# Input-projection tiles and the LRU output projection trade places as filling of a chunked RWKV-7 recurrence

## The chip, the cores and the metric

One NeuronCore of one Trainium2 chip runs the whole layer as one program. The metric is the device time of one execution in microseconds. The kernel before took 3132.44 us (median of 3 runs, 3130.93 to 3138.77).

## What is computed

The reference is one layer of a diffusion backbone. A latent of 1024 tokens and a context prefix of 256 tokens, 1024 channels each, are normalised and projected by `w_in`. Two token mixers work on the result: an RG-LRU (convolution, gates, a scan over time, 1280 channels, both directions) and an RWKV-7 recurrence (16 heads of 64, both directions, whose state after the context seeds the latent's). Each has its output projection and a gate; their sum goes through `w_out`, and a SwiGLU follows. Cut to what matters here:

```python
def merge(lru, rwkv, g_lru, g_rwkv, p):
    m = jax.nn.sigmoid(g_lru) * (lru @ p['w_o_lru']) + jax.nn.sigmoid(g_rwkv) * (rwkv @ p['w_o_rwkv'])
    return m @ p['w_out']

def mixer(h_ctx, h_lat, p, rows, need_ctx_out):
    ux_c, uy_c, zr_c, gl_c, gr_c = jnp.split(h_ctx @ p['w_in'], pts, axis=-1)
    ux_l, uy_l, zr_l, gl_l, gr_l = jnp.split(h_lat @ p['w_in'], pts, axis=-1)
    ...
    lru_l = ((hf_l + hb_l) * jax.nn.gelu(uy_l)).astype(h_lat.dtype)
    rw_c, S_c = rwkv_branch(centred_shift(zr_c, p['rwkv_mu']), S_zero, p, need_ctx_out)
    rw_l, _ = rwkv_branch(centred_shift(to_colmajor(zr_l, rows), p['rwkv_mu']), S_c, p, True)
    out_l = merge(lru_l, rw_l, gl_l, gr_l, p)
```

The columns uy (LRU gelu branch), gl and gr (the two merge gates) of the projection are needed only by `lru_l` and `merge`.

## The kernel before

All products with float32 data are made of three matmuls of a split operand (hi*hi, hi*lo, lo*hi). Channels lie on the partitions, tokens on the free axis.

The first stage (`phase_ux`, line 243) projects the ten ux tiles, then V, and runs the LRU tile by tile beside that (`lru_tiles`, line 344, an interleaved generator). The second stage (`phase_a2`, line 808) makes the RWKV operands in ten units (two for the context, eight for the latent; four operand groups each, `wkv_operands`), and the 32x32 triangular inverses of each chunk on VectorE (`wkv_inverse`, line 702: 31 steps of two instructions, tiles `it` and `X`, then transposes into `xo` and stores into `x_d`, line 740). The last unit's inverse can start only when its operands are done.

The remaining 26 tiles of the projection (10 of uy, 8 of gl, 8 of gr) need nothing but `h`. `plain` (line 289) is a generator that does one such tile per call: `inproj` (line 218) loads two halves of the weight (256 KB each, `wraw`), splits them on VectorE (line 230) and GpSimd (line 231), makes 48 matmuls of 512 columns (two weight halves, two token halves, four blocks of channels, three products; tile `pin`), and ScalarE copies the two results into `ev` (line 296), which SyncE stores (line 297). `NFILL` = 15 of these tiles stand in the first stage, the last three (`NEND`) at its end; the other 11 are spread evenly over the second stage by a due rule (line 869), 11/38 of a tile per operand group.

The recurrence (`phase_b`, line 1118) has 40 steps of 32 tokens: 0 to 7 for the context, 8 to 39 for the latent. Two halves of the heads (`wkv_chain`, line 977) take turns: products `ru` of the chunk's keys with the state, a copy, a product with the chunk's inverse `xc`, copies, products `pn` for the next state, copies (line 985, or a VectorE multiply, line 1043, on odd steps), and for latent steps the outputs `py`, copied into `ys` and stored. Every step loads 1.5 MB (`skb`, `ska`) into rings of three steps (`wkv_load`, line 965). Step 8 is the first that needs the latent's inverses (`x_d`). Context steps have a high priority in the planner (`CTXP`, `CTXO`), which otherwise orders each engine's queue by its own time model and by the order in which the program was written.

Between the chain's pieces, twice a step (`FILLAT`), the LRU output projection is put in as filling (`lru_out`, line 1053): for each half of the tokens ten tiles are prepared (load `lh` and `lu`, gelu, product on GpSimd at line 1067, split at lines 68 and 69), then for eight output tiles 30 matmuls each (tile `pol`, line 1087), 480 in all. The pace counts context steps twice, and leaves `TAIL` = 45 for after the last step. From step 28 on the group norms of the recurrence's output (`norms`) join in.

Memory pools are stacked from two edges. `h`, the weight ring (`wpool`), `ev` (`evp`) and the projection's PSUM (`psin`) stay open until the end of the second stage; the recurrence's pool `bp` then takes their place. The inverse's pool `pinv` stands at the right edge from the second context unit on.

Of the kernel before, what the change touches and what calls it, by code (L numbers as in the profile page):

```python
# [8 lines left out]
F32 = mybir.dt.float32  # L9
# [7 lines left out]
P = 128  # L17
# [265 lines left out]
NFILL = 15  # L283
# [5 lines left out]
def plain(k, start=0):  # L289

    jobs = [(UY0 + i, k.uy_d, i) for i in range(10)]
    jobs += [(GL0 + i, k.gl_d, i) for i in range(8)] + [(GR0 + i, k.gr_d, i) for i in range(8)]
    for m, dst, i in jobs[start:]:
        for o, c, w in inproj(k, m, k.psin, LAT):
            u = k.evp.tile([P, 512], F32, name=f"ev{m}_{c}", tag="ev", bufs=EVB)
            k.nc.scalar.copy(u, o)
            k.nc.sync.dma_start(dst[i * P:(i + 1) * P, c:c + w], u)
        yield

# [508 lines left out]
def phase_a2(k, hc):  # L808
# [3 lines left out]
    with tc.tile_pool(name="pprep", bufs=1) as k.prep, tc.tile_pool(name="pzr", bufs=1) as k.zrp, tc.tile_pool(name="pa2c", bufs=1) as cp, \  # L812
# [106 lines left out]
EVB = 2  # L919
# [57 lines left out]
def wkv_chain(k, a):  # L977
# [13 lines left out]
    def outputs(s, tvu):  # L991
# [6 lines left out]
        ys = k.op.tile([P, 256], F32, name=f"ys{s}_{a}", tag="ys", bufs=4)  # L998
# [97 lines left out]
FILL0 = 0  # L1096
# [21 lines left out]
def phase_b(k):  # L1118
    tc = k.tc
    k.gnp = k.root.enter_context(tc.tile_pool(name="gnp", bufs=1, side="right"))  # L1120
    with tc.tile_pool(name="bp", bufs=1) as k.bp, tc.tile_pool(name="olp", bufs=1) as op, \
            tc.tile_pool(name="psc1", bufs=1, space=PSUM) as k.psb, tc.tile_pool(name="psc2", bufs=1, space=PSUM) as k.psb2, \
            tc.tile_pool(name="pso", bufs=1, space=PSUM) as pso:
        k.bpool = k.bp
        k.op = op
        fill = lru_out(k, op, pso)
        k.pe_after = None
        done = 0
        for _ in range(FILL0):
            next(fill)  # L1130
# [5 lines left out]
        halves = [wkv_chain(k, a) for a in range(2)]  # L1136
        for s in range(NSTEP + 1):
            for i, a in enumerate((0, 0, 1, 0, 1, 1, 0, 1)):
# [15 lines left out]
                if i in FILLAT:  # L1154
                    at = s + (FILLAT.index(i) + 1) / len(FILLAT)
                    while done < (480 - FILL0 - TAIL) * (at + CTXW * min(at, 8)) / (NFEND + 8 * CTXW):
                        next(fill, None)
                        done += 1
# [7 lines left out]
        k.pe_after = None  # L1166

# [513 lines left out]
```

## Time and profile before

| | |
|---|---|
| median of 3 runs | 3132.44 us |
| the profiled execution | 3125.42 us |
| its span | 3123.3 us |
| PE, VectorE, ScalarE, GpSimd busy | 87%, 61%, 47%, 32% |
| DMA, mean over the span | 137 GB/s |

The span is that of the hardware profile; the profiled execution's own time is 2.1 us more. Busy time of PE includes the drain of each matmul, so a busy PE is not a PE at its peak. "PEclk" is TensorE's granted clock as a share of full speed.

### The profile page before, as it was taken

The numbers are of one execution on the slowest core, as the hardware profiler recorded it, in microseconds if no ns is written. First come the engines' busy times: TensorE is split into PE (matmuls) and PEld (weight loads), VectorE is DVE, ScalarE is ACT, GpSimd is POOL, SyncE is SP. The second block draws the span as 40 slices with busy tenths as digits, with TensorE's granted clock in tenths as the row PEclk, the third lists the DMA queues.
The fourth block names the chain that finished last, engine by engine and source line by source line (L and its number), as shares of the span: only waits on it lengthen the run. The fifth ranks groups of instructions, "written<-read, shape, count | busy, mean of one in ns | idle before, by whom it ended". The sixth has DMA issues, their size and how long they took to land. (4 is left out here: it accounts for less than half of the span.)

```text
span 3123.3 us, 57216 instructions
## 1 busy us (share of the span) xinstructions
PE 2730.1 (87%) x22526; PEld 2168.8 (69%) x22526; DVE 1904.5 (61%) x2841; ACT 1454.4 (47%) x2645; POOL 1011.7 (32%) x896
## 2 busy tenths in 40 slices
PE   5988888889898878887898888677899999999998
PEld 4776666767776666765665666455678888888888
DVE  7688898985567887888755233455786323232234
ACT  3476777782467555767323343344434111111114
POOL 4344444452445545666315230335441000000000
PEclk9999999999999978987558998889999999999999
DMA  5333433422555455565858787888773211111112
GB/s 204 94 117 124 121 118 117 123 69 78 152 143 140 114 123 128 129 141 130 199 137 235 227 263 225 247 235 254 258 252 110 71 54 51 41 54 42 48 56 72
DMA packets 379603, 429.19 MB, mean 137 GB/s; under 512 B 134166, under 2 KB 286150, under 8 KB 371398
## 3 DMA queue, kind: packets, MB, share of 16 engines
q1 hardware_dynamic: 379334, 425.53, 47.3%
q8 instruction: 178, 2.92, 0.4%
q14 instruction: 91, 0.75, 0.1%
HBM read 286.87 MB, written 126.26 MB: 132 GB/s over the span
## 5 line engine op out<-in xcount | busy, mean ns | idle before, releaser
L88 PE MATMUL pin<-h1024hi,whi 128*128 128x512 f32 (+1 forms) x1024 | 431.2, 421 | 58.2 <-DVE whi L230 20.4
L90 PE MATMUL pin<-h1024hi,wlo 128*128 128x512 f32 (+1 forms) x1024 | 424.4, 418 | 11.8 <-POOL wlo L231 11.4
L89 PE MATMUL pin<-h1024lo,whi 128*128 128x512 f32 (+1 forms) x1024 | 426.1, 416 | 4.1 <-DVE h1024lo L120 4.1
L231 POOL TENSOR_TENSOR wlo<-wraw,whi 128x512 fp32r<-128x512 f32 (+1 forms) x144 | 212.8, 1478 | 309.9 <-DVE whi L230 153.7
L88 PEld LDWEIGHTS pin<-h1024hi,whi 128*128 128x128 f32 (+1 forms) x1024 | 204.0, 199 | 113.1 <-DVE whi L230 21.1
L90 PEld LDWEIGHTS pin<-h1024hi,wlo 128*128 128x128 f32 (+1 forms) x1024 | 203.3, 199 | 66.9 <-POOL wlo L231 19.1
L89 PEld LDWEIGHTS pin<-h1024lo,whi 128*128 128x128 f32 (+1 forms) x1024 | 203.6, 199 | 50.8 <-DVE h1024lo L120 6.6
L54 ACT ACT_TABLE_LOAD x164 | 210.4, 1283 | 28.7 <-DMA olg<-gl_d 12.1
L982 PE MATMUL pn<-tvu,ska 128*64 128x64 f32 (+1 forms) x2496 | 165.5, 253 | 36.7 <-ACT tvu L985 22.8
L1429 DVE TENSOR_TENSOR sil<-sil,pfu 128x512 f32<-128x512 f32 x44 | 30.3, 688 | 243.6 <-PE pfu L90 243.6
L982 PEld LDWEIGHTS pn<-tvu,ska 128*64 128x64 f32 (+1 forms) x2496 | 125.0, 158 | 75.0 <-ACT tvu L985 26.9
L388 DVE SCALAR_TENSOR_TENSOR lxc<-lup,c_lru_conv_w,lxc 120x512 f32<-120x512 f32 (+3 forms) x198 | 161.0, 837 | 16.8 <-ACT lxc L386 16.2
L1437 DVE SCALAR_TENSOR_TENSOR x<-pfo,modv,x 128x512 f32<-128x512 f32 (+1 forms) x112 | 74.2, 671 | 132.3 <-PE pfo L90 132.3
L985 ACT COPY tvu<-ru 32x256 f32<-32x256 f32 x193 | 69.9, 363 | 141.1 <-PE ru L982 72.8
L68 ACT CAST whi_fi<-wraw_fi 128x1024 fp32r<-128x1024 f32 x48 | 50.6, 1053 | 168.6 <-PE pfg L89 53.3
L720 DVE TENSOR_TENSOR it<-bp,X 128x62 f32<-128x62 f32 (+25 forms) x186 | 116.6, 627 | 4.1
L230 DVE CAST whi<-wraw 128x512 fp32r<-128x512 f32 (+1 forms) x144 | 77.5, 539 | 66.0 <-PE pin L89 27.7
L721 DVE TENSOR_TENSOR X<-X,it 128x62 f32<-128x62 f32 (+25 forms) x186 | 114.3, 614 | 4.2 <-DVE it L720 0.2
L680 ACT COPY bc<-pm 32x256 f32<-32x256 f32 x160 | 98.4, 615 | 37.9 <-PE pm L676 35.4
L982 PE MATMUL ru<-tvu,skb 128*32 128x64 f32 (+1 forms) x2560 | 96.0, 242 | 21.2 <-DVE tvu L985 8.4
L982 PE MATMUL ru<-rs,xc 32*32 32x64 f32 x2560 | 87.1, 243 | 30.8 <-issue 15.7
L432 POOL TENSOR_TENSOR lxc<-la 120x512 f32<-120x512 f32 (+3 forms) x66 | 84.9, 1288 | 79.8 <-ACT la L54 68.0
(372 smaller groups left out, 7507.8 us busy)
## 6 DMA issues: line engine op xcount, KB each, us to landing
skb<-skb_d SPq DMA_DIRECT2D x40, 1024.0 KB
wraw<-in_w_in_dram SPq DMA_DIRECT2D x142, 256.0 KB
wraw_fi<-in_w_ffn_in_dram SPq DMA_DIRECT2D x48, 512.0 KB
skb_d<-kr SPq DMA_DIRECT2D x160, 128.0 KB
ska_d<-km SPq DMA_DIRECT2D x160, 128.0 KB
skb_d<-km SPq DMA_DIRECT2D x160, 128.0 KB
ska<-ska_d SPq DMA_DIRECT2D x40, 512.0 KB
wmr<-in_w_modT_dram SPq DMA_DIRECT2D x32, 512.0 KB
```

The costliest lines, as they stand in the source:

```text
L54: ins = self.nc.scalar.activation(*a, **b).ins
L88: nc.tensor.matmul(out, wh, xh, start=first, stop=False)
L89: nc.tensor.matmul(out, wh, xl, start=False, stop=False)
L90: nc.tensor.matmul(out, wl, xh, start=False, stop=last)
L230: nc.vector.tensor_copy(hi, raw)
L231: (nc.gpsimd if INLO else nc.vector).tensor_tensor(lo, raw, hi.bitcast(F32), ALU.subtract)
L388: nc.vector.scalar_tensor_tensor(xc, tap(j), k.lcw[r, t, d, j:j + 1], xc, ALU.mult, ALU.add)
L432: nc.gpsimd.tensor_tensor(xc, a, a, ALU.mult)
L680: nc.scalar.copy(bc[g, :, 4 * i:4 * i + 4].rearrange("s t e h -> s h e t"), pm[64 * c + 32:64 * c + 64, :, d, :, 32:64])
L720: nc.vector.tensor_tensor(tv, bpt[:, :, t + 1:32, t:t + 1].to_broadcast(sh), X[:, :, t:t + 1, 0:t + 1].to_broadcast(sh), ALU.mult)
L721: nc.vector.tensor_tensor(X[:, :, t + 1:32, 0:t + 1], X[:, :, t + 1:32, 0:t + 1], tv, ALU.add)
L982: k.pe_last = nc.tensor.matmul(*a, **b, start=True, stop=True).ins.name
```

## The change

Of the 26 tiles, 13 stay in the first stage (`NFILL`), none in the second stage's loop (`NMID` = 0), four are written at the end of the second stage, after the last inverse, and nine (`NLATE`) become the filling of the recurrence's steps 0 to 19 (`plain_late`, one matmul per call, with the weight's next half loaded ahead). The LRU output projection becomes the filling of steps 20 to 40 (`SWITCH`), at a pace that again leaves 45 for after them. For this `h`, `wpool` and `evp` stay open up to step 20; the projection's PSUM pool is closed before the recurrence and a new one of three banks opened at the right edge; `bp` moves to the right edge and takes in the `ys` copies; the norms' pool and the LRU output's pools open at step 20.

```diff
-NFILL = 15
+NFILL = 13
...
+NLATE = 9
+NMID = 0
+LATE = 26 - NLATE
...
+    for m, dst, i in plain_jobs(k)[start:LATE]:
+        plain_store(k, m, dst, i, inproj(k, m, k.psin, LAT))
         yield
...
+def plain_late(k):
+
+    nc = k.nc
+    jobs = plain_jobs(k)[LATE:]
+
+    def parts(m, f):
+        n = KD // 2 * P
+        raw = k.wpool.tile([P, n], F32, name=f"wraw{m}_{f}", tag="wraw", bufs=2)
+        nc.sync.dma_start(raw, k.A["w_in"][m][:, f * n:(f + 1) * n])
+        hi = k.wpool.tile([P, n], F32R, name=f"whi{m}_{f}", tag="whi", bufs=2)
+        lo = k.wpool.tile([P, n], F32R, name=f"wlo{m}_{f}", tag="wlo", bufs=2)
+        split2(nc, hi, lo, raw, nc.gpsimd)
+        return hi, lo
...
+            hi, lo = nxt
+            nxt = parts(*todo.pop(0)) if todo else None
+            for o, c, w in outs:
...
+                        ins = nc.tensor.matmul(o, a[:, r], h[b][:, kg, c:c + w], start=(kg + x == 0), stop=(kg == KD - 1 and x == 2)).ins
...
+                        yield 1
+        plain_store(k, m, dst, i, outs)
...
-                return (b + (d - b) * (x - a) / (c - a)) * (26 - NFILL)
-        return 26 - NFILL
+                    return (b + (d - b) * (x - a) / (c - a)) * NMID
+            return NMID
...
             turn(100)
+        for _ in fill:
+            pass
...
-        ys = k.op.tile([P, 256], F32, name=f"ys{s}_{a}", tag="ys", bufs=4)
+        ys = k.bp.tile([P, 256], F32, name=f"ys{s}_{a}", tag="ys", bufs=4)
...
-    k.gnp = k.root.enter_context(tc.tile_pool(name="gnp", bufs=1, side="right"))
...
+    with tc.tile_pool(name="bp", bufs=1, side="right") as k.bp, tc.tile_pool(name="psc1", bufs=1, space=PSUM) as k.psb, \
+            tc.tile_pool(name="psc2", bufs=1, space=PSUM) as k.psb2, ExitStack() as hb, ExitStack() as ho:
         k.bpool = k.bp
+        k.psin = hb.enter_context(tc.tile_pool(name="psin2", bufs=1, space=PSUM, side="right"))
+        fill = plain_late(k)
...
+            if s == SWITCH:
+                fills(48 * NLATE + 1)
+                hb.close()
+                ha.close()
+                k.gnp = k.root.enter_context(tc.tile_pool(name="gnp", bufs=1))
+                op = ho.enter_context(tc.tile_pool(name="olp", bufs=1))
+                pso = ho.enter_context(tc.tile_pool(name="pso", bufs=1, space=PSUM, side="right"))
+                fill = lru_out(k, op, pso)
+                done = 0
...
-                    while done < (480 - FILL0 - TAIL) * (at + CTXW * min(at, 8)) / (NFEND + 8 * CTXW):
+                    if s < SWITCH:
+                        fills(48 * NLATE * (at + CTXW * min(at, 8)) / (SWITCH + 8 * CTXW))
+                    else:
+                        fills((480 - TAIL) * (at - SWITCH) / (NFEND - SWITCH))
...
+SWITCH = 20
...
+        hs = ha.enter_context(ExitStack())
+        k.psin = hs.enter_context(tc.tile_pool(name="psin", bufs=1, space=PSUM))
...
+        hs.close()
+        k.root = ctx
+        k.gnbufs = 1
+        phase_b(k, ha)
```

## Rows read from the trace of the kernel before

**Rows 1.** Page, busy tenths in 40 equal slices, PE.

```profile
PE   5988888889898878887898888677899999999998
```

**Rows 2.** Busy time by stage: stretch, us, each engine (instructions), clock, DMA share, GB/s.

```profile
92.00:705.00 613.00, 532.47 (x2428) 418.32 (x2427) 505.25 (x729) 442.46 (x670) 265.52 (x236) 0.96 0.37 112
705.00:970.00 265.00, 244.40 (x1618) 195.89 (x1617) 153.13 (x241) 135.34 (x278) 107.96 (x120) 0.97 0.48 130
970.00:1453.00 483.00, 405.08 (x3356) 323.29 (x3355) 400.94 (x598) 297.06 (x582) 278.44 (x306) 0.88 0.53 124
1453.00:1690.00 237.00, 193.41 (x2247) 137.24 (x2245) 165.13 (x285) 94.71 (x193) 87.35 (x91) 0.58 0.69 184
1690.00:1862.00 172.00, 142.35 (x3191) 107.32 (x3191) 52.48 (x99) 70.96 (x150) 60.77 (x42) 0.95 0.83 247
1862.00:1955.00 93.00, 75.86 (x2104) 59.11 (x2105) 32.33 (x62) 30.20 (x72) 6.09 (x4) 0.91 0.77 224
1955.00:2143.00 188.00, 135.85 (x3122) 100.73 (x3124) 102.45 (x145) 92.24 (x236) 67.13 (x30) 0.87 0.82 230
2143.00:2300.00 157.00, 135.57 (x575) 104.15 (x568) 113.66 (x127) 59.90 (x102) 71.84 (x27) 0.95 0.89 292
```

**Rows 3.** Timelines: start us, us, engine, instruction, [idle before <-releaser].

```profile
1470.86 5.50 ACT L932 COPY ska<-c_ident 64x2048 f32<-64x2048 f32 x3 [1.20 <-DMA gr_d<-ev]
...
1485.95 1.93 PE L982 MATMUL ru<-tvu,skb 64*32 64x64 f32 x64
...
1674.30 2.06 DVE L730 STREAM_TRANSPOSE xo<-X 64x1024 f32<-64x1024 f32 x1
...
1677.51 0.54 SPq L740 DMA_DIRECT2D x_d<-xo  x1
```

**Rows 4.** Waits from 1453 to 1690: waiter <- releaser, us, times, longest.

```profile
POOL kb L652 <- PE pm L676: 54.5, 7, 15.0
```

**Rows 5.** Timeline of PE, a dense group of LRU output matmuls in step 20.

```profile
1870.82 0.40 PE L1087 MATMUL pol<-lhi,olh 128*128 128x512 f32 x1
...
1871.52 0.39 PE L1087 MATMUL pol<-lhi,olh 128*128 128x512 f32 x1
```

**Rows 6.** Groups by line on VectorE, 1453 to 1690, the recurrence's copies.

```profile
L985 DVE COPY tvu<-ru 32x256 f32<-32x256 f32 x26 | 11.0, 423 | 13.3 <-ACT tvu L985 7.7 <-PE ru L982 4.9
L1043 DVE TENSOR_TENSOR tvu<-pn,pb 64x512 f32<-64x512 f32 x16 | 11.0, 688 | 15.8 <-PE pn L982 15.4
...
L985 DVE COPY tvu<-pn 64x512 f32<-64x512 f32 x7 | 4.8, 687 | 14.3 <-PE pn L982 12.8 <-ACT tvu L985 1.3
...
L985 DVE COPY rs<-ru 128x256 f32<-128x256 f32 x7 | 3.0, 425 | 14.9 <-PE ru L982 14.8
```

**Rows 7.** Timeline of VectorE, two instructions of the last inverse.

```profile
1645.88 1.50 DVE L720 TENSOR_TENSOR it<-bp,X 128x256 f32<-128x256 f32 x1
1647.42 0.43 DVE L721 TENSOR_TENSOR X<-X,it 128x256 f32<-128x256 f32 x1
```

**Rows 8.** Tile pol (LRU output) by stage, columns as in rows 2.

```profile
1453.00:1690.00 237.00, 20.81 (x54) 12.22 (x54) 0.00 (x0) 0.58 0.69 184
1690.00:1862.00 172.00, 60.73 (x207) 37.57 (x207) 5.44 (x8) 0.95 0.83 247
1862.00:1955.00 93.00, 22.31 (x69) 12.27 (x67) 1.38 (x2) 0.91 0.77 224
1955.00:2143.00 188.00, 38.61 (x107) 22.30 (x107) 2.77 (x4) 0.87 0.82 230
```

**Rows 9.** Timeline of VectorE, the last state updates of steps 19 and 27.

```profile
1860.19 1.41 DVE L1043 TENSOR_TENSOR tvu<-pn,pb 64x512 f32<-64x512 f32 x2 [3.35 <-PE pn L982]
...
1951.25 1.41 DVE L1043 TENSOR_TENSOR tvu<-pn,pb 64x512 f32<-64x512 f32 x2 [1.52 <-PE pn L982]
```

**Rows 10.** Timeline of GpSimd, first and last product of the LRU output's preparation.

```profile
1633.11 2.64 POOL L1067 TENSOR_TENSOR lh<-lh,lu 128x512 f32<-128x512 f32 x2 [42.61 <-ACT lu L54]
...
1689.59 1.27 POOL L1067 TENSOR_TENSOR lh<-lh,lu 128x512 f32<-128x512 f32 x1 [4.06 <-DMA lh<-lru_d]
```

More of the change, by code (lines that the diff above doesn't have):

```diff
@@ L286 @@
 POFF = 400
-def plain(k, start=0):
[L291 to L297, printed above, removed]
-        yield
+NLATE = 9
+NMID = 0
+LATE = 26 - NLATE
@@ new lines, in plain_jobs, with plain_store @@
+def plain_jobs(k):
+    jobs = [(UY0 + i, k.uy_d, i) for i in range(10)]
+    return jobs + [(GL0 + i, k.gl_d, i) for i in range(8)] + [(GR0 + i, k.gr_d, i) for i in range(8)]
+def plain_store(k, m, dst, i, outs):
+    for o, c, w in outs:
+        u = k.evp.tile([P, 512], F32, name=f"ev{m}_{c}", tag="ev", bufs=EVB)
+        k.nc.scalar.copy(u, o)
+        k.nc.sync.dma_start(dst[i * P:(i + 1) * P, c:c + w], u)
+def plain(k, start=0):
+    for m, dst, i in plain_jobs(k)[start:LATE]:
+        plain_store(k, m, dst, i, inproj(k, m, k.psin, LAT))
+        yield
@@ new lines, in plain_late @@
+def plain_late(k):
[9 more added lines that the diff above has]
+        return hi, lo
+    todo = [(m, f) for m, _, _ in jobs for f in range(2)]
+    nxt = parts(*todo.pop(0))
+    for m, dst, i in jobs:
+        outs = [(k.psin.tile([P, 512], F32, name=f"pin{m}_{c}", tag="in", bufs=k.inbufs), c, w) for c, w in LAT]
+        for f in range(2):
+            hi, lo = nxt
+            nxt = parts(*todo.pop(0)) if todo else None
+            for o, c, w in outs:
+                h = k.h[0]
+                for kk in range(4):
+                    kg, r = f * 4 + kk, slice(kk * P, (kk + 1) * P)
+                    for x, (a, b) in enumerate(((hi, 0), (hi, 1), (lo, 0))):
+                        ins = nc.tensor.matmul(o, a[:, r], h[b][:, kg, c:c + w], start=(kg + x == 0), stop=(kg == KD - 1 and x == 2)).ins
+                        if k.pe_after is not None:
+                            k.tc.add_manual_dep(ins, k.pe_after, NOSYNC, reason="pace")
+                            k.pe_after = None
+                        yield 1
+        plain_store(k, m, dst, i, outs)
@@ L1115, with phase_b @@
 POOLOPS = (0, 1)
-def phase_b(k):
+def phase_b(k, ha):
     tc = k.tc
-    k.gnp = k.root.enter_context(tc.tile_pool(name="gnp", bufs=1, side="right"))
-    with tc.tile_pool(name="bp", bufs=1) as k.bp, tc.tile_pool(name="olp", bufs=1) as op, \
-            tc.tile_pool(name="psc1", bufs=1, space=PSUM) as k.psb, tc.tile_pool(name="psc2", bufs=1, space=PSUM) as k.psb2, \
-            tc.tile_pool(name="pso", bufs=1, space=PSUM) as pso:
+    with tc.tile_pool(name="bp", bufs=1, side="right") as k.bp, tc.tile_pool(name="psc1", bufs=1, space=PSUM) as k.psb, \
+            tc.tile_pool(name="psc2", bufs=1, space=PSUM) as k.psb2, ExitStack() as hb, ExitStack() as ho:
         k.bpool = k.bp
-        k.op = op
-        fill = lru_out(k, op, pso)
+        k.psin = hb.enter_context(tc.tile_pool(name="psin2", bufs=1, space=PSUM, side="right"))
+        fill = plain_late(k)
         k.pe_after = None
         done = 0
-        for _ in range(FILL0):
-            next(fill)
         with tc.high_priority(offset=SETO):
@@ L1136, in phase_b, with fills @@
         halves = [wkv_chain(k, a) for a in range(2)]
-        for s in range(NSTEP + 1):
+        def fills(n):
+            nonlocal done
+            while done < n:
+                next(fill, None)
+                done += 1
+        for s in range(NSTEP + 1):
+            if s == SWITCH:
[7 more added lines that the diff above has]
+                done = 0
             for i, a in enumerate((0, 0, 1, 0, 1, 1, 0, 1)):
@@ L1539, in tile_hybrid_block @@
             return
-    k.root = ctx
-    k.gnbufs = 1
-    phase_b(k)
+        hs.close()
+        k.root = ctx
+        k.gnbufs = 1
+        phase_b(k, ha)
     if end("b", y=k.y_d, lruh=k.lru_d, uy=k.uy_d, gl=k.gl_d, gr=k.gr_d):
```

4 lines of the change are left out of this document (removed).

## Prediction

> **What bounds the kernel now.** I read the page's slices first. TensorE (PE) is busy for nine tenths of most slices, so a gain must come from places where PE idles, waits or runs at its lower clock [rows 1]. The table by stage shows where they are [rows 2]. Its lines, in order: the first stage with the LRU (92 to 705 us), the gates and the two context units (705 to 970), the eight latent units (970 to 1453), the end of the second stage (1453 to 1690), recurrence steps 8 to 19, 20 to 27 and 28 to 39, and the hand-over to the third stage. From 705 to 970 PE sets the pace: 244 of 265 us, against 153 on VectorE (DVE). From 970 to 1453 PE (405 us) and DVE (401 us) are nearly level. From 1453 to 1690 two things run side by side: the last unit's operands and the inverses, which end on DVE at 1676 with their stores issued up to 1678, and context steps 0 to 7 of the recurrence, the first of which begins at 1486 [rows 3]. PE's granted clock is 0.58 there, so most of the stretch is at 1.2 GHz, and the two get in each other's way: GpSimd waits 54.5 us for PE's products pm of the last unit, up to 15 us at a time [rows 4]. The steps from 1690 on hold PE, DMA and, after step 28, the norms.
>
> All edits move work; the number of input-projection matmuls stays the same. One tile is 48 of them. Three pitches in a dense group take 0.70 us, 0.233 us each [rows 5], so a tile is 11.2 us of PE.
>
> **The change part by part.** The sum is against the profiled run's own 3125.4 us.
>
> *Two tiles fewer in the first stage* (15 to 13). 22 us of PE leave a stretch with PE at 532 and DVE at 505 of 613 us [rows 2]. DVE's LRU work stays and closes the stage, so little comes back: -7 (0 to -22).
>
> *Eleven tiles fewer in the second stage's loop.* By the pace rule, 11*8/38, three of them stand in the gates and context units: 34 us of PE where PE rules. -28 (-17 to -34). The other eight are 90 us in the latent units. PE falls to 315, DVE loses sixteen casts (about 10 us) and stays at 391, so DVE becomes the bound. Between the present 86% and 100% of DVE the stretch lasts 455 or 391 us instead of 483. I take 95%, 412 us, because inverse work is queued on DVE for most of that time: -71 (-28 to -92). Each moved tile also takes its two loads, casts, subtractions and copies and its two stores along; these engines have room in both places.
>
> *No more overlap of context steps and inverses.* This is the largest cost. The recurrence's pool bp now starts from the right edge, where the inverse's pool (two 8 KB buffers and one of 2 KB) and the operand pool lie; its tiles add up to 87 KB. In the kernel before, bp takes the place of the first pools, and its first fill, the copies of the identity, waited for the last store of an input tile, ev: 1470.86 us; the first ru came at 1486 [rows 3]. So by the same rule it will wait for the last store of the last inverse. Ring loads queue behind that on SP and the three copies on ScalarE; the 15 us from the copies to the first ru come after the inverse instead of beside it.
> The stretch is then four pieces. First, the inverse end: DVE is busy 165 us from 1453 to 1690, 30 of these with the recurrence's copies [rows 6], and about 10 are inverse instructions of 1.50 us where the next takes 0.43 [rows 7], while GpSimd multiplies for the LRU output, work that goes away from here. 125 us at 95%: 132 (125 to 146). Second, the last store (6) and the 15 above: 21. Third, the four remaining input tiles, 45 us: beside the inverse if their casts get through on DVE, or after it, where the 21 hide half: +8 (0 to 22). Fourth, eight context steps with 432*16/28 = 247 fills, 31 each. Steps 20 to 27 have 69 fills in 93 us, 8.6 a step of 11.6 us; steps 8 to 19 have 207 in 172 us, 17.25 a step of 14.3 [rows 2, 8, 9]. Between these a fill costs 0.31 us. With 22 more fills at the pitch of 0.233 and without the output products a step takes about 15.8: 126 us. If waits hide all fills it is 93, by 0.31 it is 148. I take 126 at the high clock, since with 8.6 fills a step the granted clock is already 0.91 [rows 2].
> 132+21+8+126 = 287 against 237: +50 (+1 to +101).
>
> *Steps 8 to 19* get 185 fills instead of 207, with no preparation to wait for: 22*0.31 = -7 (0 to -15).
>
> *Steps 20 to 40* hold all of the LRU output but its tail of 45: 435 fills where 69+107 were [rows 8], so 259 more. At 0.233 these are 60 us. PE is idle for 69 of the 281 us [rows 2], so I let half be absorbed: +30. Its first ten tiles' preparation took 56 us, GpSimd's first product at 1633 to the tenth at 1690 [rows 10]; it can start only when the last input tile is done, so some three steps have few fills and the later ones more: +5. Both halves' preparations now meet the norms on ScalarE. The LRU loads at the switch stand on SP ahead of ring loads and stores of y; the ring of three steps covers about two steps of that. DMA: 8.6 weight tiles of 1.18 MB and twenty tiles of 0.52 MB make 20.7 MB on top of 64 MB; at the 292 GB/s of the hand-over this fits in 290 us, so it sets no end before +9. Sum +35 (0 to +80, the 0.31).
> Here a rule of the Trainium skill speaks against the change. "TensorE: Matmul & The Clock Gate", Part 2, says that only weight loads are pulled ahead and matmuls stay in program order, so a fill delays the chain's next matmul by its full length. By this rule the absorbed half is paid as well, and the sum is 30 us worse; it is a rival below.
>
> *The third stage* finds its first weights' place under the LRU output's tiles instead of the ring: +4 (0 to 9). The y copies' move to bp and the norms' pool, which opens at step 20 and is first used at 28, cost nothing as long as those eight steps lie between.
>
> Sum: -7 -28 -71 +50 -7 +35 +4 = -24, that is 3101 for the profiled run. It lies 7.0 us under the median of the three runs, 3132.4, so the forecast is 3108.
>
> **The rivals.** *Slower by the lost overlap.* DVE doesn't close up when PE is relieved, since an operand chain goes through four engines: -40 instead of -71 there, 141 us to the last inverse, 17.5 us a context step, C = 141+21+8+140 = 310, +73. Total -7-28-40+73-7+35+4 = +30: 3162. For it: DVE stands idle for 82 of 483 us now, with inverse work of its own at hand [rows 2]. Against it: what it waits for is an operand chain that PE's other work holds up. It decides from a last inverse that ends about 24 us later than the 1479 us that my terms give.
> *Slower by the late steps.* The fills cost 0.31 each, as PE's order makes likely: +80 instead of +35, total +21: 3153. By the skill's rule alone it is +65, total +6.
> *Nothing to measure.* The gains and the context steps cancel: 3132. That would also be the time if the tiles were hidden anyway and the steps had room.
> *More gain.* Waits hide the fills of the context steps (93 us) and most of the late ones (+20): -33-15 on top, total -72: 3060. Against it: at 17 fills a step they already cost 0.31.
>
> **How the numbers follow.** Forecast case 0.43 (3108, own range 3080 to 3122), more gain 0.12, nothing 0.15, lost overlap 0.20, late steps 0.10. Forecast and more gain make faster 0.55; slower 0.30. A measurement of this kernel tells about 0.3%, 9 us, from no change. The half-widths of the bounds, taken as independent, are 11, 9, 32, 50, 8, 40 and 5, together 74 us; three quarters of that is 55, and the slow side is stretched over the rival at 3162: 3055 to 3168.
>
> **What would show it.** In the changed profile: the latent units' stretch near 410 us with DVE above 93%; the first ru after the last x_d store, and the last inverse near 1480; context steps of 15 to 16 us with a granted clock near 0.9; the last input tile done at step 20, and then steps of 13 to 14 us up to step 28. Wrong if context steps still begin before the inverse ends, if DVE stays under 88% with PE relieved, or if PE sits at the low clock in the context steps (then about 60 us more).

## The result: 45 us slower

| | before | after |
|---|---|---|
| median | 3131.68 us (3121.72 to 3138.77) | 3176.31 us (3167.28 to 3179.94) |
| the profiled execution's span | 3123.3 us | 3178.2 us |
| PE, VectorE, ScalarE, GpSimd busy in it | 2730, 1904, 1454, 1012 us | 2723, 1895, 1462, 1022 us |

The ratio is 1.0141 with a 95% interval of 1.0124 to 1.0158. The forecast was 3108 us, 0.8% faster; both the sign and the range were missed. The engines are as busy as before. What changed is how well the parts lie beside each other.

The same view as [rows 2], cut at the changed kernel's own marks: stretch, then busy time of PE, weight loads, VectorE, ScalarE and GpSimd with their instructions, granted clock, DMA share, GB/s (2140 to 2190 is left out).

```profile
92.00:720.00 628.00, 555.40 (x2491) 440.78 (x2491) 508.99 (x735) 442.98 (x673) 274.69 (x238) 0.93 0.36 112
720.00:970.00 250.00, 221.37 (x1629) 179.43 (x1628) 174.01 (x277) 154.53 (x316) 113.60 (x134) 0.89 0.50 128
970.00:1423.00 453.00, 353.27 (x3023) 283.98 (x3023) 395.15 (x587) 289.09 (x572) 271.18 (x295) 0.80 0.53 123
1423.00:1542.00 119.00, 24.84 (x352) 20.68 (x350) 90.73 (x182) 33.76 (x59) 37.29 (x47) 0.52 0.49 110
1542.00:1708.00 166.00, 165.49 (x1850) 118.42 (x1850) 32.53 (x64) 28.85 (x68) 12.79 (x10) 0.89 0.49 145
1708.00:1840.00 132.00, 122.45 (x3306) 94.76 (x3295) 51.99 (x101) 45.48 (x112) 7.67 (x6) 1.00 0.76 224
1840.00:2140.00 300.00, 244.15 (x4677) 181.33 (x4678) 115.98 (x177) 142.40 (x309) 139.87 (x86) 0.89 0.90 262
2190.00:2350.00 160.00, 126.61 (x555) 99.39 (x556) 106.69 (x118) 59.24 (x100) 64.87 (x25) 0.92 0.79 268
```

Read it from the fourth line down. From 1423 to 1542 us the inverses end alone, with PE at 25 of 119 us. Then come the context steps, in which PE is busy for 165 of 166 us: they are no chain with waits, they are PE work. Steps 8 to 19 follow, fast, at the high clock. Steps 20 to 36 take 300 us where they took 245.

The hand-over from the second stage to the recurrence is as the forecast had it. In the timelines, as in [rows 3], the identity copies wait for the last store of the last inverse (x_d<-xo), and the first ru follows 15 us behind that:

```profile
1524.07 2.80 SPq L786 DMA_DIRECT2D x_d<-xo  x4
...
1529.37 5.50 ACT L980 COPY ska<-c_ident 64x2048 f32<-64x2048 f32 x3 [38.84 <-DMA x_d<-xo]
...
1542.36 1.93 PE L1030 MATMUL ru<-tvu,skb 64*32 64x64 f32 x64 [53.05 <-DMA skb<-skb_d]
```

To compare stage by stage I use marks that every kernel here has. In the timeline of GpSimd, the last product kr of a unit tells when the unit's operands are nearly done (its store on SyncE can follow much later, for unit 8 of the kernel before 29 us); the last store of x_d ends the inverses; and a ring load of ska can be issued only when the step three before it is done, so that the load for step n+3 marks the end of step n. The last kr of unit 8, before and after:

```profile
1468.36 1.13 POOL L657 TENSOR_TENSOR kr<-zr,em 128x256 f32<-128x256 f32 x1
```

```profile
1404.53 1.12 POOL L703 TENSOR_TENSOR kr<-zr,em 128x256 f32<-128x256 f32 x1
```

The ends of steps 7, 19 and 36 in the kernel before:

```profile
1687.78 0.48 SPq L974 DMA_DIRECT2D ska<-ska_d  x1
...
1860.18 0.46 SPq L974 DMA_DIRECT2D ska<-ska_d  x1
...
2105.18 1.47 SPq L974 DMA_DIRECT2D ska<-ska_d  x1
```

| mark, us | before | forecast | after | blocks in order (below) |
|---|---|---|---|---|
| operands of unit 1 | 957 | 922 | 925 | 924 |
| operands of unit 8 | 1470 | 1364 | 1406 | 1404 |
| last store of the inverses issued | 1678 | 1479 | 1527 | 1525 |
| end of step 7 | 1688 | 1632 | 1708 | 1646 |
| end of step 19 | 1860 | 1797 | 1840 | 1776 |
| end of step 36 | 2105 | 2077 | 2140 | 2088 |
| end of the span | 3123 | 3099 | 3178 | 3129 |

The forecast's column is my terms added to the marks of before, with all of the +35 for steps 20 to 40 set ahead of the end of step 36. So the operands up to unit 8 gained 64 us where 106 were forecast. The context steps took 166 us after a start of 15, where 126 and 29 were forecast. Steps 8 to 19 gave 33 us more than I thought. Steps 20 to 36 took 20 more, and what lies behind them 16 more.

### The profile page after: what moved, and what is told of

It reads as the page before. It is cut to its first block, busy times and chain, and to the rows that moved or that the text cites. A ratio compares the mean times of both kernels' runs of the same rounds, so it can differ in the third digit from the quotient of the medians.

```text
span 3178.2 us, 57210 instructions
## 1 busy us (share of the span) xinstructions
PE 2722.6 (86%) x22526; PEld 2174.1 (68%) x22526; DVE 1895.3 (60%) x2841; ACT 1462.1 (46%) x2652; POOL 1022.4 (32%) x896
## 5 line engine op out<-in xcount | busy, mean ns | idle before, releaser
L88 PE MATMUL pin<-h1024hi,whi 128*128 128x512 f32 (+1 forms) x880 | 381.4, 433 | 53.8 <-DVE whi L230 12.2
L90 PE MATMUL pin<-h1024hi,wlo 128*128 128x512 f32 (+1 forms) x880 | 375.2, 429 | 14.8 <-POOL wlo L231 14.6
L89 PE MATMUL pin<-h1024lo,whi 128*128 128x512 f32 (+1 forms) x880 | 375.1, 426 | 4.1 <-DVE h1024lo L120 4.1
L88 PEld LDWEIGHTS pin<-h1024hi,whi 128*128 128x128 f32 (+1 forms) x880 | 182.0, 207 | 105.0 <-ACT h1024hi L119 12.6
L90 PEld LDWEIGHTS pin<-h1024hi,wlo 128*128 128x128 f32 (+1 forms) x880 | 181.0, 206 | 67.3 <-POOL wlo L231 24.3
L89 PEld LDWEIGHTS pin<-h1024lo,whi 128*128 128x128 f32 (+1 forms) x880 | 181.0, 206 | 47.0 <-DVE h1024lo L120 6.6
L1033 DVE COPY tvu<-ru 32x256 f32<-32x256 f32 x127 | 53.7, 423 | 145.8 <-ACT tvu L1033 81.5
L713 PE MATMUL pkt<-c_ident,kb 128*128 128x128 f32 x320 | 62.7, 329 | 73.5 <-DVE kb L696 37.4
L476 POOL TENSOR_TENSOR lg<-lg,lxc 120x512 f32<-120x512 f32 (+3 forms) x66 | 88.7, 1351 | 80.6 <-ACT lg L54 80.4
L1030 PEld LDWEIGHTS ru<-tvu,skb 128*32 128x32 f32 (+1 forms) x2560 | 59.0, 116 | 79.3 <-issue 65.8
```

Of the source, the lines that this page charges most:

```text
L88: nc.tensor.matmul(out, wh, xh, start=first, stop=False)
L89: nc.tensor.matmul(out, wh, xl, start=False, stop=False)
L90: nc.tensor.matmul(out, wl, xh, start=False, stop=last)
L476: nc.gpsimd.tensor_tensor(gi, gi, xc, ALU.mult)
L1030: k.pe_last = nc.tensor.matmul(*a, **b, start=True, stop=True).ins.name
L1033: (nc.vector.tensor_copy if k.turn % 5 in COPYD else nc.scalar.copy)(out, src)
```

## Experiments

### The context steps: what PE does in them

A stretch of PE's timeline in the changed kernel's step 4, where ru of one half and pn of the other stand in the queue in turns:

```profile
1623.98 0.31 PE L1030 MATMUL ru<-tvu,skb 128*32 128x64 f32 x4
1624.22 0.34 PE L1030 MATMUL pn<-tvu,ska 128*64 128x64 f32 x4
1624.48 0.30 PE L1030 MATMUL ru<-tvu,skb 128*32 128x64 f32 x2
1624.71 0.33 PE L1030 MATMUL pn<-tvu,ska 128*64 128x64 f32 x2
1624.97 0.30 PE L1030 MATMUL ru<-tvu,skb 128*32 128x64 f32 x2
```

Two ru and two pn take 0.49 us from start to start (1624.48 to 1624.97). Elsewhere in the same kernel 32 ru in a row take 0.58 us:

```profile
1575.16 0.65 PE L1030 MATMUL ru<-tvu,skb 128*32 128x64 f32 x32
1575.74 0.50 PE L339 MATMUL pin<-h1024lo,whi 128*128 128x512 f32 x1
```

The planner puts the products in turns since both halves have one precedence. In the program's order of PE's instructions the small products of steps 1 to 7 change from one tile to another 280 times.

**e1: blocks in order.** Every product of a block is tied to the end of the block before it, in steps 0 to 7 alone.

```diff
     def mm(*a, **b):
-        k.pe_last = nc.tensor.matmul(*a, **b, start=True, stop=True).ins.name
+        ins = nc.tensor.matmul(*a, **b, start=True, stop=True).ins
+        if k.block is not None:
+            k.tc.add_manual_dep(ins, k.block, NOSYNC, reason="block")
+        k.pe_last = ins.name
...
+                k.block = k.pe_last if s < CTXP and (s, i) > (0, 0) else None
```

> The changed kernel, with one thing more: in the context steps 0 to 7 each block of the recurrence's small products (16 or 32 of ru, pn or the product with xc) is made to follow the block before it, so that the blocks of the two halves no longer alternate product by product in PE's order. Nothing else is moved. Theory A (alternation): the context steps of the changed kernel last 163 us for eight, 20.4 each, because pairs of ru and pn alternate at some 0.24 us a pair where 32 of one kind in a row take 0.6 us; then the eight steps fall to 95 to 115 us and the run to 3105 to 3130. Theory B (fills): the 31 input matmuls a step set the 20 us; then the eight steps stay above 150 us and the run within 10 us of 3176.

Measured: 3126.5 us, ratio to the kernel before 0.9999 (0.9990 to 1.0009). The 45 us are gone by this edit alone. The first line is the context steps of e1, the second steps 8 to 19:

```profile
1537.00:1646.00 109.00, 105.12 (x1816) 80.13 (x1817) 32.28 (x64) 28.85 (x68) 12.87 (x10) 0.96 0.77 232
1646.00:1776.00 130.00, 123.17 (x3327) 95.35 (x3327) 51.96 (x101) 44.98 (x111) 7.66 (x6) 1.00 0.78 225
```

From the first ru (1540) to the end of step 7 that is 106 us instead of 166, with the same 31 fills a step. Changes of tile fall from 280 to 52. By groups of PE's instructions, pn of the changed kernel from 1600 to 1700 and of e1 from 1545 to 1645 (busy, mean ns of one):

```profile
L1030 PE MATMUL pn<-tvu,ska 128*64 128x64 f32 x332 | 35.8, 238 | 0.0
```

```profile
L1030 PE MATMUL pn<-tvu,ska 128*64 128x64 f32 x430 | 16.6, 225 | 0.0
```

A pn costs 0.108 us of PE in turns and 0.039 in a row. The Trainium skill, "TensorEngine Tiling (Array Packing)", section Key Properties, says that a change of tiling mode drains TensorE. The two kinds have unlike shapes in these rows, 128*32 and 128*64, and the trace agrees. From the rows the price of a change is (0.49 - 0.11) / 2, some 0.19 us, where 0.11 is two ru and two pn in a row; 228 changes fewer make 43 of the 60 us. The rest is not accounted for; the granted clock rose as well, from 0.89 to 0.96. It is the change of shape that costs, not that of the tile: in e1's latent steps ru and py, both 128*32, stand in turns too, and two of each take 0.06 us:

```profile
1706.65 0.23 PE L1030 MATMUL ru<-tvu,skb 128*32 128x64 f32 x2
1706.67 0.25 PE L1030 MATMUL py<-tvu,skb 128*32 128x64 f32 x2
1706.71 0.23 PE L1030 MATMUL ru<-tvu,skb 128*32 128x64 f32 x2
```

**e2: the same in the kernel before.**

> The kernel before with the same order of blocks in its context steps. If alternation costs PE time there too, but the inverse on DVE ends the stretch (1676 us), little comes of it: 0 to -20 us, 3110 to 3132. If PE, at its lower clock, is what holds the inverse and the context steps up there, the stretch of 237 us shortens by 30 to 60 us: 3070 to 3100. If alternation costs nothing: 3132.

Measured: 3122.1 us, 0.9978 (0.9963 to 0.9993). So the order is worth 2 to 12 us there. Its context steps do get shorter: step 7 ends at 1618 instead of 1688. But step 8 needs the last inverse, whose load comes behind the last x_d store:

```profile
1617.54 0.56 SPq L974 DMA_DIRECT2D ska<-ska_d  x1
...
1660.19 1.01 SPq L740 DMA_DIRECT2D x_d<-xo  x2
...
1663.84 0.80 SPq L970 DMA_DIRECT2D xc<-x_d  x2
```

The change took the cover away from a cost that had been there all the time.

### The lost overlap

**e3: the kernel before with only the pool moved.**

```diff
-    with tc.tile_pool(name="bp", bufs=1) as k.bp, tc.tile_pool(name="olp", bufs=1) as op, \
+    with tc.tile_pool(name="bp", bufs=1, side="right") as k.bp, tc.tile_pool(name="olp", bufs=1) as op, \
```

> The kernel before with only the recurrence's pool moved to the right edge, so that its context steps wait for the last inverse; no tile and no output product is moved. Theory A (the lost overlap costs): the undisturbed inverse ends near 1570 to 1590, the first ru comes 15 to 20 us later and eight context steps of 15 to 20 us follow, against 1690 now: +40 to +80, 3170 to 3210. Theory B (the overlap was worth nothing, since the two got in each other's way at PE's lower clock): within 10 us of 3132.

Measured: 3146.2 us, 1.0061 (1.0046 to 1.0076), +19 us. The move didn't do all that the expectation says. The context steps don't wait for the last inverse: the identity copies begin behind an earlier store of x_d, and the first ru comes 19 us ahead of the last store. In the kernel before it is 192 us ahead, so nine tenths of the overlap are gone, not all of it.

```profile
1582.69 5.49 ACT L932 COPY ska<-c_ident 64x2048 f32<-64x2048 f32 x3
...
1596.36 1.93 PE L982 MATMUL ru<-tvu,skb 64*32 64x64 f32 x64 [35.98 <-DMA skb<-skb_d]
...
1613.13 2.85 SPq L740 DMA_DIRECT2D x_d<-xo  x4
```

The inverses, less disturbed, end at 1616 instead of 1678, step 7 at 1730 instead of 1688, but step 36 at 2107, level with before: no bunch of output products stands in steps 8 and 9 now. In the steps, then, the lost overlap comes back. The loss lies behind step 36: in the profiles 10 us up to the last output product, and 11 from there to the last stage's first product, in the hand-over, where 22 us lie between the last output product and the third stage's first (1.6 before).

**e10: e3 with blocks in order and the third stage's pools on the right edge.** Nothing else of the change is in it.

```diff
-    k.wpool = pool(name="wpoolc", bufs=2)
+    k.wpool = pool(name="wpoolc", bufs=2, side="right")
...
-    k.hap = pool(name="hap", bufs=1)
+    k.hap = pool(name="hap", bufs=1, side="right")
```

> The kernel before with the recurrence's pool on the right edge (the run of the lost overlap, 3146 us), with the blocks in order in steps 0 to 7 and the third stage's pools on the right edge; no tile and no output product is moved. Theory A (what the move to the right edge costs is the alternation, now uncovered, and the hand-over, and not the overlap as such): context steps at 12 us instead of 15 (-25) and the hand-over -15: 3100 to 3112, faster than the kernel before. Theory B (the overlap itself is worth its 20 us): 3125 to 3140.

Measured: 3125.1 us, 0.9988 (0.9970 to 1.0005): by the number the second theory's range. The step marks speak for the first: step 7 ends at 1706 instead of 1730 and step 36 at 2087 instead of 2107. (The first ru is again 19 us ahead of the last x_d store.) The last stage had become 13 us longer, for a reason of its own (e13, e14).

### The second stage

**e4: 15 tiles in the first stage, two at the tail** (`NFILL = 15` in the changed kernel).

> The changed kernel with 15 instead of 13 input tiles in the first stage, so two instead of four at the second stage's tail. Theory A (VectorE's LRU work closes the first stage, PE time there is free): the first stage stays within 5 us and the second stage ends up to 22 us earlier: 3154 to 3172. Theory B (the tiles cost the same in either place): within 5 us of 3176. My forecast's term was +7 in the first stage and -4 at the tail.

Measured: 3203.7 us, 1.0247 (1.0230 to 1.0265), 27 us slower than the changed kernel. Both theories fall. The operands of unit 1 come 17 us later (942): the two tiles taken out of the first stage had given 17 us, not the 7 of my term. Units 2 to 6 then lose another 12 with no work added there, which I can't explain, and units 7 to 9 gain 14 without two of the tail's tiles, which so had not been hidden. The inverses end 22 us later.

**e8: junk in the latent units.** e1 with 336 products in units 2 to 8 that nobody reads.

```diff
                 turn(1 if u + 1 < NUNIT else LASTN)
+                if 2 <= u < 9:
+                    junk = k.psin.tile([P, 512], F32, name=f"junk{u}_{i}", tag="in", bufs=k.inbufs)
+                    hh = k.h[0][0]
+                    for q in range(12):
+                        nc.tensor.matmul(junk, hh[:, q % 8, 0:P], hh[:, q % 8, 512:1024], start=q == 0, stop=q == 11)
```

> The run with blocks in order, with 336 products on PE whose result nobody reads, 48 in each of the units 2 to 8 (seven input tiles' worth, 78 us at 0.233, without their loads, casts, subtractions, copies and stores). Theory A (clock: PE, relieved, waits more and falls to its low clock more often, 0.80 instead of 0.88, and so the gain in the latent units was 45 instead of 71 us): the junk raises the clock to 0.86 or more and the last product kr of unit 8 is stored within 10 us of 1408. Theory B (PE's time counts as such): 1445 to 1490, as in the kernel before (1487).

The stretch of the latent units, first of e1, then of e8:

```profile
929.00:1410.00 481.00, 375.31 (x3290) 301.94 (x3289) 421.61 (x626) 309.00 (x609) 286.74 (x317) 0.82 0.53 122
```

```profile
929.00:1410.00 481.00, 412.78 (x3462) 333.20 (x3462) 398.71 (x606) 302.67 (x596) 270.96 (x303) 0.87 0.51 115
```

The last kr of unit 8 is stored at 1428, between the two theories. (Their 1408 and 1487 are stores as well; 1487 is that of the thirteenth kr in the kernel before, the sixteenth follows at 1499.) By the products themselves, 78 us of PE cost 18 net of where unit 1 stood. The clock rose from 0.82 to 0.87. So PE's time there is mostly free, and relieving PE lowers its clock. From unit 1's operands to unit 8's the kernel before takes 512 us and e1 480. In the traces 257 fewer products of input tiles (pin) stand between these marks in e1, and not the 384 of eight tiles, since the tail's four tiles ran here: their results are stored from 1345 to 1430. At 18 us for 336 products some 14 of the 33 us are PE's; the others I put down to the work beside them. VectorE stays at 88% of the stretch (422 of 481 us), not at 95.

### The late steps

**e5: no output products in steps 20 to 40** (`TAIL = 480` in e1).

> The run with blocks in order (3127 us), with all 480 products of the LRU output after the last step instead of 435 of them in steps 20 to 40. It tells what steps 20 to 40 take without them: from the ring loads of step 19 to those of step 36 these steps take 312 us with them and 245 in the kernel before with its 8.6 a step. Theory A (the fills cost what they hold PE for, 0.233 to 0.31 us each): without them 180 to 215 us. Theory B (loads, norms and the chain set the late steps): 250 to 300 us. The run itself ends later, since some 112 us of fills then stand alone: 3100 to 3180.

**e12: junk products in their place.** A generator with the same interface yields products of one constant tile, 22 a step; the output products all follow the last step.

```diff
-                fill = lru_out(k, op, pso)
+                rest = lru_out(k, op, pso)
+                fill = junk(k, op, pso)
...
+            ins = nc.tensor.matmul(p, jr[:, 0:P], jr, start=True, stop=True).ins
```

> The run without output products in steps 20 to 40, with as many products (22 a step) whose result nobody reads in their place: PE is held as long, but there are no loads, casts, gates and stores beside it; the output products all follow the last step, so the run itself ends late, 3180 to 3230. From the ring loads of step 19 to those of step 36: 263 us without fills, 312 with the output products. Theory A (a fill's PE time is nearly free, since it keeps the clock up, and what costs is the work beside the output products): 225 to 260 us with a granted clock of 0.95 or more. Theory B (22 fills a step cost through PE's order): 295 to 330 us.

**e15: junk products, and beside them the output projection's own work** (loads, preparation, casts, gates, stores; 24 of its 30 products a tile are left out).

```diff
                 next(fill, None)
+                if rest is not None:
+                    next(rest, None)
...
+                    if i not in (0, 9):
+                        yield 1
+                        continue
```

> The run with 22 junk products a step in steps 20 to 40, and beside them the LRU output's own loads, preparation, casts, gates and stores at their usual pace, with 6 of its 30 products a tile (the other 24 are left out). The junk has a buffer of its own, so it doesn't wait for the preparation; no step has over 42 fills in PE's order but the 21st. From the ring loads of step 19 to those of step 36: 312 us with the output products, 258 with junk alone. Theory A (the work beside the products costs: transfers, ScalarE, GpSimd): 285 to 320 us. Theory B (bunches of 106 fills and the waits for the preparation cost): 255 to 275 us.

Steps 20 to 36 of, in this order, e1 (with the output products), e5 (without), e12 (junk) and e15 (junk and the work beside):

```profile
1776.00:2088.00 312.00, 257.56 (x4829) 190.50 (x4827) 120.07 (x182) 146.94 (x320) 143.66 (x88) 0.89 0.91 257
```

```profile
1782.00:2045.00 263.00, 170.11 (x4321) 135.45 (x4318) 105.41 (x169) 99.40 (x249) 78.60 (x45) 0.73 0.84 242
```

```profile
1781.00:2039.00 258.00, 221.20 (x4737) 172.28 (x4737) 104.74 (x166) 101.69 (x252) 77.73 (x45) 0.93 0.85 239
```

```profile
1784.00:2079.00 295.00, 250.77 (x4831) 190.84 (x4830) 122.29 (x182) 147.36 (x317) 146.57 (x92) 0.92 0.91 271
```

22 products a step cost nothing that shows (258 us against 263), and with them the granted clock is 0.93 instead of 0.73. Each of e5, e12 and e15, as e8, is a single execution, and with late steps written as in e1 the same stretch takes from 300 (the changed kernel) to 316 us (e13), so a gain of 5 us is not shown. The work beside the output products adds 37 us (258 to 295): 45 us more on ScalarE, 69 more on GpSimd, DMA from 0.85 to 0.91. In e15 the gates' and the products' buffers are single and the six real products a tile still wait for the preparation, so the 37 hold such waits too. The last 17 us (295 to 312) may be how the products lie: in e1's order of instructions they wait for their preparation and then stand in steps 27 and 28 with 40 and 106 at once. They are about as large as the spread of that stretch, so this is not shown. The runs themselves took 3215.2 (e5) and 3216.8 us (e12), with the output products standing alone at the end, and 3116.4 (e15).

**e7: blocks in order in all steps** (`CTXP = 41` in e1), which spreads these bunches; the most in one step is 42.

> The run with blocks in order (3127 us), with the same order and the chain's precedence over the fills in all steps instead of 0 to 7. In PE's order the most fills in one step of 20 to 38 fall from 106 to 42, since they now stand only where the chain leaves room. Theory A (bursts cost: 40 and 106 fills in steps 27 and 28 hold both halves for 9 and 25 us): 30 to 50 us off the late steps, 3080 to 3100. Theory B (the number of fills costs, not how they lie): within 10 us of 3127.

Measured: 3125.4 us, 0.9990 (0.9972 to 1.0008). Steps 20 to 36 take 300 us, 12 less than e1 and as long as in the changed kernel, and no gain in the run can be told from none: most of the loss isn't in the bunches.

**e6: the switch at step 12** (`SWITCH = 12` in e1), and **e11: five late tiles, four in the second stage's loop, the switch at step 8** (`NLATE = 5`, `NMID = 4`, `SWITCH = 8` on e7, with e10's pools).

> The run with blocks in order (3127 us), with the switch at step 12 instead of 20: 432 input matmuls in steps 0 to 11, 43 a context step, and 435 output products over 28 steps, 15.5 a step instead of 21.75. Theory A (the late fills are too dense; at 15 a step, as in steps 8 to 19 now at 10.8 us, they are nearly free): context steps +20 to +25 us, the rest -30 to -60: 3090 to 3120. Theory B (what costs in the late steps is the stop at the switch and the burst after it, whatever the density): the loss moves to steps 12 to 20 and stays as large, with the context steps on top: 3140 to 3155.

> The run with blocks in order in all steps (3125 us) and the third stage's pools on the right edge, with five instead of nine late tiles (four more in the second stage's loop) and the switch at step 8: 240 input matmuls in the context steps, 30 a step, then 435 output products at 13.6 a step. If the density of late fills is what costs (21.75 a step now, 13.6 here): steps 8 to 39 lose 30 to 50 us, the second stage gains 20 to 28, the hand-over -15: 3080 to 3105. If four tiles in the second stage cost as much as the late steps give back: 3110 to 3130.

Measured: 3139.7 us, 1.0038 (1.0019 to 1.0057), and 3137.3 us, 1.0027 (1.0014 to 1.0041). Steps 22 to 27 of e6, ahead of the norms, have 17 output products each in the trace and take 15 us; with 15.4 input products e1's steps 8 to 19 take 10.8. From the end of step 7 to the end of step 36 e6 takes 433 us and e11 424; e1 takes 442, the changed kernel 433 and e7 432. So spreading them thinner gives back little, which fits that the work beside the products moves along. What it gives is lost elsewhere: the context steps end 26 us later in e6 than in e1, the inverses 27 us later in e11, and e11 also carries the 13 us of the next section.

### The hand-over and an odd 13 us

In the kernel before, the third stage's first weights are loaded at 2144.65, ahead of the last output product (2154.65), and its first product por comes 1.6 us behind that. In the changed kernel the loads wait for the output products' tiles (last pol 2202.60), and por starts at 2221.42. The loads of before and after, and what PE waits for after:

```profile
2144.65 0.84 SPq L80 DMA_DIRECT2D wraw_or<-in_w_o_rwkv_dram  x2
```

```profile
2211.66 0.83 SPq L80 DMA_DIRECT2D wraw_or<-in_w_o_rwkv_dram  x2
...
PE prw L1333 <- DMA r0lo<-rw_d: 17.7, 1, 17.7
```

**e9: e1 with e10's pools.**

> The run with blocks in order (3127 us), with the third stage's weight pool and input pool opened from the right edge, so that they lie where the recurrence's pool was and not where the output products' tiles are. Theory A (the hand-over: there 18.6 us lie between the last output product and the first product of the third stage, 1.6 in the kernel before, because the weights' loads wait for the output products' tiles): that gap falls under 6 us and the run to 3109 to 3118. Theory B (the gap is filled with norms' work that would then come later): within 6 us of 3127.

Measured: 3133.8 us, 1.0022 (1.0004 to 1.0039). The gap fell to 4 us, and the run became 7 us longer. The cause stands in PE's timeline of the last stage, where PE doesn't wait: from its first product to the end it takes 762 us in e9 and 748 in e1. e1, then e9:

```profile
2599.11 0.39 PE L88 MATMUL pfu<-h1hi,whi_fi 128*128 128x512 f32 x1
2599.34 0.39 PE L89 MATMUL pfu<-h1lo,whi_fi 128*128 128x512 f32 x1
2599.56 0.39 PE L90 MATMUL pfu<-h1hi,wlo_fi 128*128 128x512 f32 x1
2599.79 0.39 PE L88 MATMUL pfu<-h1hi,whi_fi 128*128 128x512 f32 x1
```

```profile
2599.04 0.39 PE L88 MATMUL pfu<-h1hi,whi_fi 128*128 128x512 f32 x1
2599.27 0.39 PE L89 MATMUL pfu<-h1lo,whi_fi 128*128 128x512 f32 x1
2599.50 0.39 PE L90 MATMUL pfu<-h1hi,wlo_fi 128*128 128x512 f32 x1
2599.74 0.39 PE L88 MATMUL pfu<-h1hi,whi_fi 128*128 128x512 f32 x1
```

0.68 us for three products against 0.70, at a granted clock of 1.00 in both. All of the stage's pfu and pfg have this pitch (0.2267 and 0.2333 us in the mean); pfo has 0.2267 in both. By the memory maps of the two kernels, the weights and the inputs of these products in e1 both begin 32 bytes behind a multiple of 128; in e9 the weights begin 96 behind one, the inputs 32.

**e13 and e14: e9 and e10 with a pad of 64 bytes**, so that the two begin alike again.

```diff
+    pool(name="padc", bufs=1, side="right").tile([P, 16], F32, name="padc")
     k.wpool = pool(name="wpoolc", bufs=2, side="right")
```

> The run with blocks in order and the third stage's pools on the right edge (3134 us), with a pad of 64 bytes a partition at the right edge ahead of them, so that the third stage's weights and inputs lie at the same distance from a multiple of 128 bytes. Theory A (the pitch of a product depends on how its two operands lie to each other): the last stage's products come at 0.2265 us again and the run loses 13 us, 3117 to 3123; against 3127 without the hand-over's mending that leaves 4 to 10 us for the hand-over. Theory B (it is the place far up in the memory, or something else): 3134 within 5.

> The kernel before with the recurrence's pool on the right edge, the blocks in order and the third stage's pools on the right edge (3125 us), with the same pad of 64 bytes. Theory A (how the operands lie): 3109 to 3116, 0.4 to 0.6% faster than the kernel before. Theory B: 3125 within 5.

Measured: 3121.8 us, 0.9979 (0.9959 to 0.9998), and 3114.3 us, 0.9957 (0.9940 to 0.9973). The pitch is back: the last stage takes 748 us again, and the runs are 12 and 11 us shorter. Against e1, e13 shows what the hand-over itself cost: 6 us by the ratios, whose intervals allow anything from none to 13. Closing the gap of 18.6 us gives so little because PE's waits mostly move: between the last output product and the last stage's first product PE idles for 32 us in e1 and still for 24 in e13. e14, the kernel before with the recurrence's and the third stage's pools moved, ordered blocks and a pad, beats both kernels without moving a single tile.

**e16 and e17: a pad of 96 bytes ahead of the input projection's weights** in the kernel before and in e14.

```diff
+        ha.enter_context(tc.tile_pool(name="padw", bufs=1)).tile([P, 24], F32, name="padw")
         k.wpool = ha.enter_context(tc.tile_pool(name="wpool", bufs=2))
```

> The kernel before with a pad of 96 bytes a partition ahead of the input projection's weight pool, and nothing else, so that its weights and the inputs of the latents lie at the same distance from a multiple of 128 bytes. Theory A (how the operands lie sets the pitch, here too): products in a dense group come at 0.2265 instead of 0.233 us, and of the 2640 products of 128x512 up to 17 us come back, less where VectorE rules: 3115 to 3128. Theory B (something else set the third stage's pitch): pitch 0.233 and 3131 within 5.

> The fastest kernel so far (the kernel before with the recurrence's pool on the right edge, blocks in order, the third stage's pools on the right edge and the pad of 64 bytes, 3114 us) with the same pad of 96 bytes ahead of the input projection's weights. Theory A: 3098 to 3111. Theory B: 3114 within 5.

Measured: 3125.2 us, 0.9989 (0.9973 to 1.0004), and 3112.2 us, 0.9961 (0.9945 to 0.9978). No gain in time that can be told from none. The pitch did follow, though. A dense group of e16:

```profile
299.74 0.39 PE L88 MATMUL pin<-h1024hi,whi 128*128 128x512 f32 x1
299.97 0.39 PE L89 MATMUL pin<-h1024lo,whi 128*128 128x512 f32 x1
300.19 0.39 PE L90 MATMUL pin<-h1024hi,wlo 128*128 128x512 f32 x1
300.42 0.39 PE L88 MATMUL pin<-h1024hi,whi 128*128 128x512 f32 x1
```

Over all neighbouring products of an input tile that follow each other without a wait, the mean from start to start falls from 0.233 us (the kernel before, e14) to 0.229 (e16, e17); most come at 0.226 or 0.227 now, the others at up to 0.24. That is some 11 us of PE, and the run doesn't get shorter by it. A like distance from 128 bytes so counts here too, but isn't the whole rule; which it is stays open.

## Why the prediction was wrong, point by point

Three terms failed: the latent units, the context steps and steps 20 to 40.

*First stage, gates and context units* (-35 together): right, -32. The split was off; e4 puts 17 into the first stage, where I had 7.

*Latent units* (-71): the step that failed is VectorE closing up to 95%. It stayed at 87% (395 of 453 us; 88% in e1), and the units gave 32, from unit 1's operands to unit 8's. It had been busy for 83% before (401 of 483), not for the 86% that I started from. e8 shows why PE's relief gives little: PE's time there was mostly free, and the clock sinks when it is taken out (0.88 to 0.80). Part of the miss is the tail's tiles, which ran here and not behind the inverses: five tiles' worth of products left this stretch, not eight. That was the rival of the lost overlap, in its words: DVE doesn't close up.

*The inverses' end* (1479): 48 us late; 42 of these stand already in unit 8's mark. From there to the last store it took 121 us, where my terms leave 115.

*The start and the tail's tiles* (+29): 15 us for the start, as forecast; the tiles had run before it.

*Context steps* (126): 166. With the latent units this is the largest miss, 40 us, and the mechanism was not among my terms or rivals. I took a step's own PE work from latent steps and added fills at their pitch. The context steps' products stand in the queue in another order, in turns, and every change of shape costs some 0.19 us. I had read their slowness in the kernel before as the low clock and the inverses beside them. e1 shows the cost: with ordered blocks the eight steps take 106 us, better than my 126.

*Steps 8 to 19* (-7): 172 us became 132, a gain of 40. The price of 0.31 us a fill was read from a stage's mean that held a stall. Tile pol in the kernel before (columns as in [rows 8]):

```profile
1690.00:1740.00 50.00, 30.58 (x110) 20.91 (x110) 3.36 (x5) 0.93 0.71 210
1740.00:1862.00 122.00, 30.16 (x97) 16.66 (x97) 2.08 (x3) 0.96 0.88 262
```

110 of the 207 fills stand in the first two of twelve steps, behind the late preparation [rows 10]. The other ten steps have 9.7 each and take 12.2 us, hardly more than steps 20 to 27 with 8.6.

*Steps 20 to 40* (+35): 55 up to step 36 and 68 up to the last output product. The rival of the late steps (+80) came nearer, for the wrong reason. The Trainium skill ("TensorE: Matmul & The Clock Gate", Part 2) says that matmuls stay in program order. From that I had concluded that a fill is paid in full, and half of the fills made my +30. No run here speaks against the order, but 22 junk products a step cost nothing that shows (e12). The room is there without them: PE is busy for 170 of 263 us in e5, and its longest waits are for the chain's copies (pn for tvu 17.7 us, ru for rs 11.4). The work beside the products costs 37 us, and I had put it at next to nothing ("sets no end before +9", and 5 for the preparation). So what the +35 got right of the size is luck. Whether ScalarE, GpSimd or the transfers are what slows the chain there was not tried apart.

*The third stage* (+4): right in size, 7 us from the last output product to the end (976 us against 969), though the gap itself was 18.8 us.

*The rivals.* The lost overlap named its point of decision, a last inverse 24 us later than 1479, and it came 48 later; its sum of 3162 falls short mostly by the turns in the context steps, 166 us where it had 140. But the overlap as such was not what the time went to. Step 8 needs the last inverse with it or without, and e14, with a tenth of the overlap left and the blocks in order, is faster than the kernel before. A kernel with none of it left and nothing else moved was not run.

## What to carry to other kernels

Before an overlap is given up, look at what it covers: a queue that is busy all the time, as PE in the context steps, may be full of avoidable cost that nobody paid for so far, and its instruction order tells it. A price per instruction taken from a stage's mean is good only if the stage holds no stall; look at two halves of it first. And for filling in a chain that waits on copies, count the loads, casts and stores that come with it, not the matmuls.

## What was not expected of the hardware

- Small products of 128*32 and 128*64 in turns cost TensorE 0.19 us a change in the changed kernel, ten times one of them in a row (0.018 us for a ru). Products of two tiles that have one shape, 128*32, take turns at no such price (two of each in 0.06 us, e1).
- Products of 512 columns follow each other at 0.2265 or 0.233 us at the full clock, depending on where in SBUF their two operands begin; 64 bytes of padding in the third stage are worth 11 to 12 us of 3125 (e9 to e13, e10 to e14).
- A chain of small products without filling runs at a granted clock of 0.73 and takes 263 us (e5, steps 20 to 36); with 22 idle products a step it runs at 0.93 and takes no longer, 258 (e12).
